# Rotating images by 90 degrees: loads of 16 rows to a partition, two images alternating on a quadrant's partitions, in slabs of 2 MB

## The chip, the cores and the metric

One core of a Trainium2 chip runs the kernel; the launch names no other. The metric is the device time of one execution in microseconds (us). Medians of several runs are given. "Span" is the length of the profiled execution, about 1.8 us less than the time of the same run.

## The reference

```python
x = np.random.randn(32, 3, 256, 256).astype(np.float32)      # 25.17 MB
out = np.rot90(x, k=-1, axes=(-2, -1))                       # out[.., i, j] = x[.., 255 - j, i]
```

Nothing is computed. Every byte is read once and written once, and each of the 96 images is transposed with one axis reversed.

## The kernel before

```python
R = 8; G = H // R                      # 8 rows of an image on a partition; 32 partitions = 1 image
n_slabs = B * C * G // P               # 24 slabs of 4 images, 1 MB
PARTS = 2; CP = R // PARTS
ld_v = x.rearrange("b c h w -> (b c h) w").rearrange("(n p r) w -> n p (r w)", p=P, r=R)
st_v = out.rearrange("b c h w -> (b c h) w").rearrange("(n p c) w -> n p (c w)", p=P, c=R)
in_pool = ...bufs=12
out_pool = ...bufs=12

for n in range(n_slabs):
    t_in = in_pool.tile([P, R * W], fp32, tag="t_in")
    nc.sync.dma_start(out=t_in, in_=ld_v[n])              # 128 partitions x 8 KB
    t_out = out_pool.tile([P, R * W], fp32, tag="t_out")
    src = t_in.rearrange("p (r g c) -> p c r g", r=R, c=R)
    dst = t_out.rearrange("p (c g r) -> p c r g", c=R, r=R)[:, :, ::-1, ::-1]
    for k in range(PARTS):
        cs = slice(k * CP, (k + 1) * CP)
        nc.vector.transpose(out=dst[:, cs], in_=src[:, cs])   # 32x32 blocks on VectorE
    nc.scalar.dma_start(out=st_v[n], in_=t_out)           # 128 partitions x 8 KB
# ... (cut: imports, launch)
```

As the kernels use it, a transpose on VectorE swaps 32 partitions (called a quadrant here) with 32 elements of a partition. Here the 32 partitions are the 32 groups of 8 rows of one image, and the 32 elements are one column out of each of 32 groups of 8 columns, 32 bytes apart. So an output partition receives 8 whole output rows, 8 KB in one piece. In the traces no load or store is issued before the last one on its completion semaphore has landed; from the second use of a semaphore on, a load's issue starts 16 to 81 ns after that landing. Loads and stores use four semaphores each once stores run, so at most four loads and four stores are in flight. (At the very start five loads were issued before one had landed.)

## Time and profile before

| | before |
|---|---|
| time, median of 3 runs | 124.81 us |
| span of the profile | 122.9 us |
| VectorE busy | 94.6 us |
| data packets | 3072 loads and 3072 stores of 8 KB, 309 ns nearly all |
| end of the last load packet | 110.6 us |
| first packet, end of the last packet | 1.80 us, 121.61 us |

The packet counts and times are from the trace's record of each DMA packet. Below are lines of the page of the kernel before. DVE is VectorE. The first three are the 40 slices of the span (busy tenths of VectorE, busy tenths of the DMA engines, GB/s); then the two queues (q1 loads, q10 stores: packets, MB, share of 16 engines' span); then the chain of waits by engine; then the group of the transposes (count, busy us, mean ns of one, idle before it and what ended it).

```profile
DVE  0199999999897697796977967979769779797500
...
DMA  2999999999999999999999999999999999999994
GB/s 93 427 427 403 339 424 427 427 429 427 427 432 427 427 427 427 432 429 427 427 427 427 429 427 427 427 427 429 427 427 427 427 429 427 427 429 427 427 424 171
...
q1 hardware_dynamic: 3456, 25.17, 49.2%
q10 hardware_dynamic: 3456, 25.17, 48.5%
...
DMA 89%; DVE 2%; DVEq 2%; SPq 1%; issue 0%
...
L51 DVE STREAM_TRANSPOSE t_out<-t_in 128x1024 f32<-128x1024 f32 x48 | 94.6, 2052 | 20.9 <-DMA t_in<-in_x_dram 15.4
```

What to see: the DMA engines are at 9 tenths in every slice but the first and the last, at 427 GB/s nearly everywhere, while VectorE has gaps. The two queues together take 97.7% of the span. The waits of VectorE say the same (columns: who waited for what, us in total, times, longest):

```profile
DVE t_out L51 <- DMA t_in<-in_x_dram: 15.4, 12, 5.7
```

The arithmetic is short: 6144 packets x 309 ns / 16 engines = 118.7 us out of a span of 122.9 us. Only what makes packets cheaper, or the unused ends shorter, can shorten this kernel.

### The profile page before, as it was taken

The page shows a single profiled execution, that of the slowest core. Times are in us where ns is not written, and L with a number is a line of the kernel's source. Part 1 is how long each engine was busy: PE and PEld are TensorE (multiplying, and loading weights), DVE is VectorE, ACT ScalarE, POOL GpSimd, SP SyncE. Part 2 cuts the span into 40 slices and gives each one's busy share as a digit, 9 for nine tenths or more (in the row PEclk, how much of TensorE's full clock was granted, in tenths as well). Part 3 has the DMA queues.
Part 4 walks back from the last instruction along what each step waited for, and adds up shares of the span by engine and source line. Part 5 has one row for each costly group of instructions (what it writes and reads, how often), then busy time and mean ns, then how long its engine had stood idle before and what let it go on. Part 6 is the DMA issues. An engine that isn't in the chain of part 4 may idle for free.

```text
span 122.9 us, 186 instructions
## 1 busy us (share of the span) xinstructions
DVE 94.6 (77%) x48; POOL 0.2 (0%) x4
## 2 busy tenths in 40 slices
DVE  0199999999897697796977967979769779797500
POOL 0000000000000000000000000000000000000000
DMA  2999999999999999999999999999999999999994
GB/s 93 427 427 403 339 424 427 427 429 427 427 432 427 427 427 427 432 429 427 427 427 427 429 427 427 427 427 429 427 427 427 427 429 427 427 429 427 427 424 171
DMA packets 6913, 50.34 MB, mean 410 GB/s; under 512 B 768, under 2 KB 768, under 8 KB 768
## 3 DMA queue, kind: packets, MB, share of 16 engines
q1 hardware_dynamic: 3456, 25.17, 49.2%
q10 hardware_dynamic: 3456, 25.17, 48.5%
q14 instruction: 1, 0.01, 0.0%
HBM read 25.17 MB, written 25.17 MB: 410 GB/s over the span
## 4 chain that ended last, share of the span: by engine, by line
DMA 89%; DVE 2%; DVEq 2%; SPq 1%; issue 0%
DMA t_in<-in_x_dram 89%; DVE t_out L51 2%; DVEq L79 2%; SPq L44 1%; DVEq L51 0%
## 5 line engine op out<-in xcount | busy, mean ns | idle before, releaser
L51 DVE STREAM_TRANSPOSE t_out<-t_in 128x1024 f32<-128x1024 f32 x48 | 94.6, 2052 | 20.9 <-DMA t_in<-in_x_dram 15.4
L68 POOL MEMSET const-uint8-127<- 128x1 uint8 x1 | 0.1, 102 | 0.0
L68 POOL MEMSET const-bfloat16-1.0<- 128x1 bf16 x1 | 0.1, 101 | 0.0
L68 POOL MEMSET const-float32-0.0<- 128x1 f32 x1 | 0.1, 98 | 0.2 <-issue 0.2
L68 POOL MEMSET const-float32-1.0<- 128x1 f32 x1 | 0.1, 98 | 0.0
## 6 DMA issues: line engine op xcount, KB each, us to landing
t_in<-in_x_dram SPq DMA_DIRECT2D x24, 1024.0 KB, 19.6
out_dram<-t_out ACTq DMA_DIRECT2D x24, 1024.0 KB, 16.5
```

What stands on the lines that cost most here:

```text
L44: nc.sync.dma_start(out=t_in, in_=ld_v[n])
L51: nc.vector.transpose(out=dst[:, cs], in_=src[:, cs])
L68: nc = _bacc.Bacc("TRN2", target_bir_lowering=False, num_devices=1)
L79: with _tile.TileContext(nc) as tc:
```

## The change

The intent is fewer and larger load packets. Sixteen rows of an image lie in one piece of 16 KB, so a partition is loaded by one packet of 16 KB. An image then takes only 16 partitions, and since a quadrant has 32, two images share it, on alternating partitions. Each load therefore writes every second partition, 64 in all. After the transpose, the two images' pixels alternate along the free axis, and the output access pattern sorts them into two halves of the output tile. Stores stay at 8 KB a partition.

```diff
-    R = 8
-    G = H // R
-    n_slabs = B * C * G // P
-    PARTS = 2
-    CP = R // PARTS
+    RI, RO = 16, 8
+    K, G = H // RI, H // RO
+    I = 2
+    Q = P // (K * I)
+    n_slabs = B * C // (Q * I)
...
+    ld_v = ...rearrange("(n i m r) w -> n i m (r w)", i=I, m=Q * K, r=RI)
+    st_v = ...rearrange("(n i p c) w -> n i p (c w)", i=I, p=P, c=RO)
-    in_pool = ...bufs=12        # the same for out_pool
+    in_pool = ...bufs=6
...
-        t_in = in_pool.tile([P, R * W], fp32, tag="t_in")
-        nc.sync.dma_start(out=t_in, in_=ld_v[n])
+        t_in = in_pool.tile([P, RI * W], fp32, tag="t_in")
+        for i in range(I):
+            nc.sync.dma_start(out=t_in[i::I], in_=ld_v[n, i])
...
+        t_out = out_pool.tile([P, I, RO * W], fp32, tag="t_out")
+        src = t_in.rearrange("p (r g c) -> p c r g", r=RI, c=RO)
+        dst = t_out.rearrange("p i (c k r) -> p c r k i", c=RO, r=RI)[:, :, ::-1, ::-1, :]
+        for c in range(RO):
+            nc.vector.transpose(out=dst[:, c], in_=src[:, c])
-        nc.scalar.dma_start(out=st_v[n], in_=t_out)
+        for i in range(I):
+            nc.scalar.dma_start(out=st_v[n, i], in_=t_out[:, i])
```

More of the change, by code (lines that the diff above doesn't have):

```diff
@@ L29 @@
     P = nc.NUM_PARTITIONS
-    R = 8
-    G = H // R
-    n_slabs = B * C * G // P
-    PARTS = 2
-    CP = R // PARTS
-    ld_v = x.rearrange("b c h w -> (b c h) w").rearrange("(n p r) w -> n p (r w)", p=P, r=R)
-    st_v = out.rearrange("b c h w -> (b c h) w").rearrange("(n p c) w -> n p (c w)", p=P, c=R)
-    in_pool = ctx.enter_context(tc.tile_pool(name="in_pool", bufs=12))
-    out_pool = ctx.enter_context(tc.tile_pool(name="out_pool", bufs=12))
-    for n in range(n_slabs):
-        t_in = in_pool.tile([P, R * W], fp32, tag="t_in")
-        nc.sync.dma_start(out=t_in, in_=ld_v[n])
-        t_out = out_pool.tile([P, R * W], fp32, tag="t_out")
-        src = t_in.rearrange("p (r g c) -> p c r g", r=R, c=R)
-        dst = t_out.rearrange("p (c g r) -> p c r g", c=R, r=R)[:, :, ::-1, ::-1]
-        for k in range(PARTS):
-            cs = slice(k * CP, (k + 1) * CP)
-            nc.vector.transpose(out=dst[:, cs], in_=src[:, cs])
-        nc.scalar.dma_start(out=st_v[n], in_=t_out)
+    RI, RO = 16, 8
[3 more added lines that the diff above has]
+    n_slabs = B * C // (Q * I)
+    ld_v = x.rearrange("b c h w -> (b c h) w").rearrange(
+        "(n i m r) w -> n i m (r w)", i=I, m=Q * K, r=RI)
+    st_v = out.rearrange("b c h w -> (b c h) w").rearrange(
+        "(n i p c) w -> n i p (c w)", i=I, p=P, c=RO)
+    in_pool = ctx.enter_context(tc.tile_pool(name="in_pool", bufs=6))
+    out_pool = ctx.enter_context(tc.tile_pool(name="out_pool", bufs=6))
+    for n in range(n_slabs):
+        t_in = in_pool.tile([P, RI * W], fp32, tag="t_in")
[8 more added lines that the diff above has]
+            nc.scalar.dma_start(out=st_v[n, i], in_=t_out[:, i])
 _INS = ['x']
```

## The prediction

> **What bounds it now.** The DMA engines. The page's 40 slices show DMA at 9 tenths from the second to the last but one, at 424 to 432 GB/s; the two queues took 49.2% and 48.5% of the 16 engines' span. Almost every 8 KB packet took 309 ns, so 6144 packets on 16 engines are 118.7 us; the rest is about 4 us of start, slow early packets and end, and 1.9 us by which the time exceeds the profile's span. The chain of waits agrees: 89% is load DMA. VectorE is busy 94.6 us (77%); its idle time (20.9 us) is mostly waiting for loads. Back to back, 128x1024 transposes start 1.907 us apart.
>
> In every 4 us window loads and stores move equally many packets (about 104)[...].
>
> **What changes.**
> 1. Bytes, DMA count (24 loads, 24 stores of 1 MB), pool bytes and DMAs in flight stay.
> 2. Load packets become 16 KB, half as many. 8 KB in 309 ns is 26.5 GB/s[...].
> 3. [...] Loads run ahead, stores lag; the total stays. The store backlog at the end (VectorE finishing near 105 us) hides the larger last slab (8 us of transposes, 4.9 us of stores). Worth about 0.
> 4. VectorE: 96 transposes of 512 elements per partition instead of 48 of 1024; [...]97 us in all, off the path. The first transpose waits for 2 MB: about 8 us instead of 5.7, off the path too.
> 5. The transposes' writes alternate between two halves 8 KB apart, then step 64 bytes, instead of stepping 32 bytes. If a write costs the same, nothing follows. There is little room: about 8 us per 2 MB slab now, and by my sum (8 + 12 slabs + 5 for the last stores + 3) VectorE binds above about 9 us.
> 6. Each load writes every second partition. [...]
>
> **Prediction.** 125.0 us, essentially unchanged; 123.4 to 142 should hold it 8 times in 10. Faster by over 2%: 0.06; within 2%: 0.56; slower by over 2%: 0.38. The long upper side is points 5 and 6.
>
> **What would show it.** Right: DMA at 9 tenths to the end; 16 KB load packets at about 610 ns, store packets at 309; loads done near 85 to 100 us, then stores alone at about 427 GB/s; transposes 0.95 to 1.05 us apart; the chain ending in store DMA. Wrong by 5: transposes over 1.13 us apart, VectorE busy nearly all of the span, DMA slices below 9, VectorE as the chain. Wrong by 6: load packets much above 618 ns while GB/s falls in the first slices, where loads run alone. Wrong by 3: a DMA gap before the last two stores. If packets of 16 KB are cut to 8 KB or less, points 2 and 3 vanish and the result stays near 125.
>
> **What would make it wrong.** A write-side penalty of the transposes with the 8 KB alternation (over 12%), [...]or loads stalling on buffers while too few stores are queued.

In point 2 is a saving of 0.8 us; with it the sum of the forecast came to 124.8 - 0.8 = 124.0 us, and the point of 125.0 leaned upward from there. The loads and stores are equal in packets on average only (0.998:1): from 20 to 104 us of the trace 96 to 114 load packets and 97 to 113 store packets end in each.

## The result, and the profile after

| | before | after |
|---|---|---|
| time, median of 6 runs | 124.83 us | 124.55 us |
| span of the profile | 122.9 us | 122.9 us |
| VectorE busy | 94.6 us | 96.3 us |
| load packets | 3072 of 8 KB, 309 ns | 1536 of 16 KB, 611 ns |
| busy per DMA engine (sum of packets / 16) | 119.98 us | 119.48 us |
| end of the last load packet | 110.6 us | 85.5 us |
| first packet, end of the last packet | 1.80, 121.61 us | 2.04, 121.73 us |

The ratio is 0.9979, with a 95% interval of 0.9966 to 0.9992. (A ratio here is the mean time of one kernel's fast runs over that of the other's of the same rounds, so it is not quite the ratio of the medians.) The time is the same within 2%; the small gain is clear of zero. The single profiled execution does not show it: its span equals that of before, and two profiles of the changed kernel, this one and a later one (122.6 us), differ by more than the gain. The outputs are right.

The same lines of the page, after:

```profile
DVE  0029999999999999999999999999999999000000
...
DMA  3999999999999999999999999999999999999993
GB/s 85 427 427 427 427 427 365 400 437 413 424 448 432 413 427 451 429 389 435 424 461 437 408 427 437 427 424 421 427 427 429 429 427 427 427 427 427 427 427 139
...
q1 hardware_dynamic: 1920, 25.17, 48.8%
q10 hardware_dynamic: 3456, 25.17, 48.5%
...
DMA 58%; DVE 23%; DVEq 1%; issue 1%; SPq 0%; ACTq 0%
...
L53 DVE STREAM_TRANSPOSE t_out<-t_in 128x512 f32<-128x512 f32 x96 | 96.3, 1092 | 8.4 <-DMA t_in<-in_x_dram 8.4
```

and the same view of VectorE's waits:

```profile
DVE t_out L53 <- DMA t_in<-in_x_dram: 8.4, 1, 8.4
```

What to see: the DMA line is the same as before, 9 tenths from end to end, and that is the result. What changed is the order. VectorE now runs without a gap from 8 us to 105 us (it waits once, for the first slab), then has nothing left to do, while the DMA engines are still at 427 GB/s with stores alone. The chain of waits now gives VectorE 23% instead of 2%; the experiments show below that this is not a bound.

### The profile page after: what moved, and what is told of

The parts are those of the page before. It is cut to its first block, busy times and chain, and to the rows that moved or that the text cites. A ratio compares the mean times of both kernels' runs of the same rounds, so it can differ in the third digit from the quotient of the medians.

```text
span 122.9 us, 225 instructions
## 1 busy us (share of the span) xinstructions
DVE 96.3 (78%) x96; POOL 0.2 (0%) x4
## 3 DMA queue, kind: packets, MB, share of 16 engines
q1 hardware_dynamic: 1920, 25.17, 48.8%
q10 hardware_dynamic: 3456, 25.17, 48.5%
HBM read 25.17 MB, written 25.17 MB: 410 GB/s over the span
## 4 chain that ended last, share of the span: by engine, by line
DMA 58%; DVE 23%; DVEq 1%; issue 1%; SPq 0%; ACTq 0%
DMA out_dram<-t_out 53%; DVE t_out L53 23%; DMA t_in<-in_x_dram 6%; DVEq L82 1%; SPq L47 0%; ACTq L56 0%; DVEq L53 0%
## 5 line engine op out<-in xcount | busy, mean ns | idle before, releaser
L53 DVE STREAM_TRANSPOSE t_out<-t_in 128x512 f32<-128x512 f32 x96 | 96.3, 1092 | 8.4 <-DMA t_in<-in_x_dram 8.4
```

The source lines that it names most:

```text
L53: nc.vector.transpose(out=dst[:, c], in_=src[:, c])
```

## The experiments

"Wrong on purpose" means that rows land in other places than the reference wants, while sizes, counts and instructions stay as told.

### 1. Only the transposes cut in two

```diff
 # kernel before
-    PARTS = 2
+    PARTS = 4
```

> The kernel before with only its transposes cut into 48x2 of 512 elements per partition (four per slab), writes still stepping 32 bytes. Theory: the fixed cost of an instruction alone explains the spacing after the change, so back-to-back starts are about 1.00 us apart (1001 ns after the change, 1907/2 = 954 plus 47). VectorE busy about 96 us, time 124.8 (124.6 to 125.0), since it is off the path. Rival: the 8 KB alternation of the writes costs something; then this kernel's spacing is clearly below 1001 ns, near 954 to 980.

Measured: 124.75 us, ratio to before 0.9993 (0.9978 to 1.0008). Back-to-back starts are 984 ns apart. The page's group line:

```profile
L51 DVE STREAM_TRANSPOSE t_out<-t_in 128x512 f32<-128x512 f32 x96 | 97.0, 1104 | 18.7 <-DMA t_in<-in_x_dram 13.1
```

That is between the theory (1001) and the rival (954 to 980): of the 47 ns, cutting costs 984 - 1907/2 = 30 ns an instruction, and the remaining 17 ns (1001 in the changed kernel) belong to the new shape. Whether its alternating writes cause them was not tested apart. In experiment 3 the writes alternate too, but the reads alternate between two images 16 KB apart and step 64 bytes instead of 32; there the starts are 920 ns apart (VectorE busy 89.4 us). So the pattern of the reads, or of both sides together, can matter more than these 17 ns. A VectorE busy time 2 us longer (97.0 against 94.6) moved nothing, as it should off the path. The prediction's cost of cutting was a guess, and too high; 30 ns is what was measured.

### 2. The change with load packets of 8 KB

```diff
 # changed kernel; wrong result on purpose
-        "(n i m r) w -> n i m (r w)", i=I, m=Q * K, r=RI)
+        "(n i b m r) w -> n i m b (r w)", i=I, m=Q * K, b=2, r=RI // 2)
...
-            nc.sync.dma_start(out=t_in[i::I], in_=ld_v[n, i])
+            nc.sync.dma_start(out=t_in[i::I].rearrange("p (b f) -> p b f", b=2), in_=ld_v[n, i])
```

> The changed kernel, with each load's 16 KB per partition read as two pieces of 8 KB from places far apart in the source (wrong result on purpose; everything else as changed). Theory (the packet size is what saves, and what moves the sharing): load packets of 8 KB at 309 ns, busy time per engine up by 0.67 us, loads and stores again equal in packets, loads end near 110 us instead of 85.5, VectorE starved again; time 125.2 (124.9 to 125.6), because at 1:1 the stores still lag by the 7.8 MB loaded before the first store, 18 us, enough to hide the last slab. Rival A (the saving comes from slab size or order, not packets): time stays at 124.55. Rival B (run-ahead[...] is needed to hide the larger last slab): a gap in DMA at the end and 126.5 us or more.

Measured: 125.24 us, ratio to before 1.0034 (1.0021 to 1.0048). Load packets are 8 KB at 309 ns; the engines' busy time is 120.35 us instead of 119.48; loads and stores are equal in bytes again (0.997 between 24 and 104 us and 0.998 before; the changed kernel has 1.79 between 24 and 84 us, while loads last); loads end at 104.7 us, not near 110 as expected. The slices and the waits:

```profile
DVE  0029999999999999999994994994995997798000
...
DMA  3999999999999999999999999999999999999993
```

```profile
DVE t_out L53 <- DMA t_in<-in_x_dram: 16.8, 6, 8.6
```

VectorE has gaps again, waiting for loads, while the DMA line stays full. So the packet size gives the saving and moves the sharing; with 8 KB packets the rest is a small loss (the first packet came at 2.19 us instead of 1.80 before; 0.15 us of that is this variant's own, since the changed kernel has 2.04). And the slab of 2 MB is hidden at its end even at 1:1: rival B falls.

### 3. 16 KB packets on both sides

Two more images share each input partition, so that a transposed block has two images on its output partitions too, with 16 output rows each.

```diff
 # changed kernel
-    RI, RO = 16, 8
+    RI, RO = 16, 16
-    I = 2
+    I, J = 2, 2
-    n_slabs = B * C // (Q * I)
+    n_slabs = B * C // (Q * I * J)
-        "(n i m r) w -> n i m (r w)", i=I, m=Q * K, r=RI)
+        "(n i j m r) w -> n i j m (r w)", i=I, j=J, m=Q * K, r=RI)
-        "(n i p c) w -> n i p (c w)", i=I, p=P, c=RO)
+        "(n i j m c) w -> n i j m (c w)", i=I, j=J, m=Q * G, c=RO)
     # both pools: bufs=3; t_in is [P, J, RI * W]
-            nc.sync.dma_start(out=t_in[i::I], in_=ld_v[n, i])
+            for j in range(J):
+                nc.sync.dma_start(out=t_in[i::I, j], in_=ld_v[n, i, j])
-        src = t_in.rearrange("p (r g c) -> p c r g", r=RI, c=RO)
+        src = t_in.rearrange("p j (r g c) -> p c r g j", r=RI, c=RO)
-            nc.scalar.dma_start(out=st_v[n, i], in_=t_out[:, i])
+            for j in range(J):
+                nc.scalar.dma_start(out=st_v[n, i, j], in_=t_out[j::J, i])
```

> Loads and stores both of 16 KB a partition: two images alternate on the input partitions and two more share each partition, so that output partitions hold 16 rows too; slabs of 4 MB, 3 + 3 buffers. Theory: packets of 611 ns on both queues, another 0.67 us less engine time, sharing 1:1; loads end later than 85.5; time 123.9 (123.6 to 124.2). Rival (the larger slab exposes its start or its end[...]): no gain or worse, 124.6 to 128, with a gap in DMA or store packets clearly over 618 ns.

Measured: correct, 124.26 us, ratio to before 0.9964 (0.9946 to 0.9981). Both kinds of packet take 611 ns, and the busy time per engine is 118.86 us: 0.62 us less than the change, as expected. The time gained only about half of that (0.29 us by the medians), just outside the range. To settle it, the two ran again on one chip, five rounds each:

> The changed kernel again, as the partner of the next run on the same chip: 0.2 to 0.4 us under the kernel before.

> 16 KB on both sides again, on the same chip as the changed kernel. Theory (0.6 us less engine time, of which 0.49 us was seen at the last packet): 0.3 to 0.6 us under the changed kernel, 0.6 to 0.9 us under the kernel before. Rival: no difference from the changed kernel beyond 0.1 us.

Measured in these rounds: before 124.70 us, changed kernel 124.52 us (ratio 0.9985, 0.9971 to 0.9999), 16 KB on both sides 124.24 us (ratio 0.9961, 0.9946 to 0.9976). It beats the changed kernel by 0.28 us and the kernel before by 0.46 us, both less than I expected (0.3 to 0.6 and 0.6 to 0.9). One reason is that the sum of the packets' times overstates the saving. Sixteen engines that each took 309 ns for one 8 KB packet after another would move 424.2 GB/s. With each packet's bytes spread over its own time, the records of the kernel before give 427.5 GB/s between 40 and 80 us. So records of successive packets overlap by about 0.8% (the DMA share reads 1.01 in that window), and the rate is the better measure. With 16 KB on both sides it is 430.6 GB/s (90 to 118 us, in both profiles). At these rates 25.17 MB of loads, or of stores, take 0.43 us less with 16 KB packets, not 0.67; this is an estimate. What became of the rest (0.43 against 0.28 us) was not settled.

### 4. Load packets of 32 KB, and the same cut to 8 KB

```diff
 # changed kernel
-    RI, RO = 16, 8
+    RI, RO = 32, 8
-    I = 2
+    I = 4
     # slabs of 4 MB, so both pools: bufs=3
```

> Loads of 32 KB a partition (four images alternating, four loads of 32 partitions a slab), stores still 8 KB; slabs of 4 MB, 3 + 3 buffers. Theory: load packets of 32 KB at about 1213 ns, 0.35 us less engine time than the change[...]; time 124.2 (123.9 to 124.6). Rivals: packets are capped at 16 KB or less (time 124.5); or loads run into their three buffers and DMA falls idle before stores exist (time over 125).

Measured: correct, 128.53 us, ratio 1.0286 (1.0261 to 1.0312). The packets are not capped: 32 KB take 1213 ns. But the time is 4 us worse. The slices and the waits:

```profile
DVE  0000899999999999998079999169999999991000
...
DMA  4799898999899999989999999999999999916995
GB/s 165 331 496 444 382 496 351 475 496 331 351 418 426 416 426 418 475 380 426 393 431 426 442 442 403 421 423 439 424 421 434 423 421 436 423 41 248 413 421 240
```

```profile
DVE t_out L53 <- DMA t_in<-in_x_dram: 13.3, 1, 13.3
DVE t_out L53 <- issue: 8.3, 2, 4.4
```

The second rival (an idle DMA) has the right sign, but names the wrong place and cause. The DMA hole is near the end, at 111 to 114 us (41 GB/s in that slice). VectorE stood still twice, 8.3 us in all. The waits view calls that "issue", which names no releaser. The chain of waits in order of time (start, length, what) and the timeline from 60 us on (start, length, what, idle before) tell more:

```profile
30.37 33.65 DMA out_dram<-t_out
...
64.04 19.43 DMA out_dram<-t_out
```

```profile
64.20 15.59 DVE L53 STREAM_TRANSPOSE t_out<-t_in 128x1024 f32<-128x1024 f32 x8 [4.42 <-issue]
83.65 31.04 DVE L53 STREAM_TRANSPOSE t_out<-t_in 128x1024 f32<-128x1024 f32 x16 [3.87 <-issue]
```

Store DMAs end at 64.02 and 83.47 us, and transposes start 0.2 us after each; at the second of these the last load had landed 6 us before. So VectorE waited for output buffers that slow stores held. By 76 us only 6.0 MB had been stored. To see whether the packets or the 4 MB slabs did that, the same kernel ran with each load cut into 8 KB pieces:

```diff
 # the 32 KB kernel; wrong result on purpose
-        "(n i m r) w -> n i m (r w)", i=I, m=Q * K, r=RI)
+        "(n i b m r) w -> n i m b (r w)", i=I, m=Q * K, b=4, r=RI // 4)
     # and the load's destination viewed as "p (b f) -> p b f", b=4
```

> The kernel with 32 KB loads and 4 MB slabs, each load now read as four pieces of 8 KB from places far apart in the source (wrong result on purpose). Theory (in the 32 KB kernel [...]VectorE stood still for output buffers, 8.3 us, and the stores ran dry at the end): with packets 1:1 VectorE no longer waits for output buffers, no DMA gap near 110 us, engine time as in the 8 KB variant of the change; time 125.3 (124.9 to 125.9) instead of 128.5. Rival (the 4 MB slabs with three buffers cause the stall): about 128.5 again.

That the stores lagged is shown by the 6.0 MB above.

Measured: 124.88 us, ratio to before 1.0007 (0.999 to 1.0023).

```profile
DVE  0000699999999999999999999999945999940000
...
DMA  2999999999999999999999999999999999999993
```

```profile
DVE t_out L53 <- DMA t_in<-in_x_dram: 13.4, 1, 13.4
DVE t_out L53 <- issue: 3.1, 1, 3.1
```

By 76 us, 9.2 MB had been stored, the hole is gone, and VectorE ended at 109.5 us instead of 114.7. So it was the packets. The theory was not exact: a wait of 3.1 us for output buffers stays, but it comes early enough to cost nothing, and the time fell slightly below my range.

### 5. Loads on 64 neighbouring partitions

```diff
 # changed kernel; wrong result on purpose
-            nc.sync.dma_start(out=t_in[i::I], in_=ld_v[n, i])
+            nc.sync.dma_start(out=t_in[i * (P // I):(i + 1) * (P // I)], in_=ld_v[n, i])
```

> The changed kernel with each load on 64 neighbouring partitions (0 to 63, then 64 to 127) instead of every second one; wrong result on purpose, same bytes and packets. [...]load packets while loads run alone take about 1200 ns instead of 611 and the DMA moves about 214 GB/s there; time well above the change, 140 us or more. Rival[...]: packets stay at 611 ns and the time at 124.5.

The theory's figures stand for half the rate of the changed kernel's loads, and the half was the author's estimate.

Measured: 165.81 us, ratio 1.3302 (1.3228 to 1.3376). Where loads run alone, the rate is half. The windows of 4 to 16 us (from:to, length, VectorE, POOL, clock, DMA share, GB/s), first of the changed kernel, then of this one:

```profile
4.00:16.00 12.00, 7.64 (x8) 0.00 (x0) 1.00 1.01 429
```

```profile
4.00:16.00 12.00, 2.79 (x3) 0.00 (x0) 1.00 1.05 218
```

218 GB/s is half (51%) of the changed kernel's 429. The load packets between 8 and 16 us take 1258 ns on average instead of 611. Note that the DMA share reads full in both (1.01 and 1.05), so a packet's time in the trace grows as the rate falls, and a full DMA line does not prove a full rate. With stores beside them the rate is still only 303 GB/s (40 to 80 us). So the alternation is what keeps the change from being a large loss. Why neighbouring partitions halve the rate was not shown.

### 6. More VectorE work on purpose

```diff
 # changed kernel; the result stays right
-        for c in range(RO):
+        for c in list(range(RO)) + [0] * 1:      # then * 2
```

> The changed kernel with one transpose of each slab done twice: 9 instead of 8 per slab, so about 9.0 us a slab. Theory (VectorE is off the path with 8, and binds just about 9): VectorE ends at 8.4 + 12 x 9.0 = 116.5 us of the span, then 2 MB of stores: time 126 (124.5 to 127). Rival (VectorE is already on the path, as the 23% in the chain of waits may suggest): plus 12 us, 136.5.

> The same with two transposes of each slab done twice: 10.0 us a slab. Theory: VectorE binds; it ends at 8.4 + 12 x 10.0 = 128.5 us, then 4.9 us of stores and about 3 us of issue and completion, plus 1.7: time 138 (136.5 to 139.5); DMA slices fall below 9 in the second half. Rival (VectorE on the path from the start): 148.5, plus 24.

Measured: with 9 transposes a slab 125.88 us, ratio 1.0093 (1.0078 to 1.0108); with 10, 139.90 us, ratio 1.1214 (1.1198 to 1.1231). The slices of the first, then of the second:

```profile
DVE  0039999999999999999999999999999999999600
...
DMA  3999999999999999999999999999999999999495
GB/s 85 423 423 423 433 433 370 412 439 402 433 444 433 418 420 447 425 415 433 444 415 423 441 436 420 423 449 404 423 428 431 425 428 431 425 428 428 188 415 222
```

```profile
DVE  0059999999999999999999999999999999999900
...
DMA  3999999999999999999999999999997076086086
GB/s 119 423 442 418 433 414 354 437 418 437 425 418 440 428 425 430 433 433 418 421 440 435 416 442 416 423 425 435 425 425 330 0 321 288 0 342 266 0 359 250
```

Twelve more transposes are about 12 us of VectorE work and cost 1.3 us; the next twelve cost 14 us. That is a bound that takes over. In the first run VectorE ends at 116.8 us and the last store packet at 122.85 us, 6.06 us later; in the second it is 130.67 and 136.7 us, 6.04 us later (and 1.2 us more to the end of the span in each). The DMA-bound end is 121.7 us, so by estimate (121.7 less these 6.0) VectorE may end up to 115.7 us of the span before it costs anything; in the changed kernel it ends at 104.7 us. Over 12 slabs that is a margin of 0.9 us on 8.0. The second run fell 0.4 us outside my range, because a slab took 10.2 us instead of the 10.0 I had reckoned with. And the 23% of the chain of waits did not mean that VectorE was on the path: with it, the first run would have taken 12 us more.

### 7. Fewer input buffers

```diff
 # changed kernel
-    in_pool = ...bufs=6
+    in_pool = ...bufs=2        # then 3
```

> The changed kernel with 2 input buffers of 2 MB instead of 6. Theory: the two buffers are full at 11.9 us, and no load can start until the first slab's transposes end at 16.4 us, and no store until then either: a DMA gap of about 4.5 to 5.5 us near the start, which is never made up; afterwards DMA is busy and the time is 129.5 (128.5 to 131). It shows that a larger slab is harmless only while loads can fill the DMA during the first slab. Rival: the gap is made up later and the time stays within 1 us of 124.5, which would mean that DMA work is not the bound.

Measured: 139.09 us, ratio 1.1131 (1.1057 to 1.1205). The expected gap is there, but the expected size is far off.

```profile
DVE  0059999159999059999129999408999808999900
...
DMA  4995099999999999998999999899989999999486
GB/s 105 429 448 238 0 305 329 462 396 453 405 408 343 441 450 396 422 322 334 410 441 422 422 343 379 362 429 427 400 343 334 346 398 439 450 405 419 181 360 250
```

```profile
DVE t_out L53 <- DMA t_in<-in_x_dram: 21.9, 4, 8.3
DVE t_out L53 <- DMA out_dram<-t_out: 11.4, 2, 5.8
```

My theory had one gap and then a full DMA line. In fact DMA stalls recur: over the run the engines are idle for at least 8.3 us between packets (the time from first to last packet less the sum of their times), and their packets take 6.6 us more in sum per engine than in the changed kernel (load packets 661 ns on average, store packets 324). VectorE waits for loads (21.9 us) and for output buffers (11.4 us).

> The changed kernel with 3 input buffers instead of 6 (2 gave 139). Theory: three buffers are filled just when the first slab's transposes end, 16.4 us, so no first gap; and a slab's load then has two slabs of transposes, 16 us, to land, so VectorE never waits for it: time 124.6 (124.3 to 125.2). Rival (any loss of run-ahead costs): between 126 and 135.

Measured: 125.79 us, ratio to before 1.0091 (1.0074 to 1.0108), against 124.52 us for six buffers on the same chip. That lies between the theory's range and the rival's. The slices:

```profile
DMA  2999999999999999999999999999999999999993
GB/s 79 429 423 429 429 357 333 392 373 437 423 437 423 442 431 434 423 423 410 437 423 429 439 450 402 445 418 445 410 431 423 426 423 429 431 426 423 426 434 161
```

VectorE waits once, for the first slab, exactly as with six, and the DMA line has no gap, but the rate dips (333 GB/s in one slice). Still it is 1.27 us slower. Of that, 0.87 us per engine are longer packets (120.26 us busy against 119.39): between 16 and 24 us, when loads resume and stores begin together, load packets average 717 ns and store packets 381 ns. Why packets stretch when traffic of both kinds begins at once was not settled. Both kernels pay some of it (the load packets' excess over their usual time sums to 0.86 us per engine before, and to 1.06 and 0.97 us in the two profiles after).

## Why the prediction was right

The time, 124.55 us, lies in the range, in the class predicted ("within 2%"), 0.45 us below the point. Point by point:

1. **Bytes, DMA count, DMAs in flight unchanged.** Right, apart from six loads instead of five at the very start, and up to six stores instead of four at the end.
2. **Larger packets save 0.8 us.** The direction is right (experiment 2: 125.24 us with 8 KB load packets against 124.55). The size, an estimate, was about twice too large. The packets' own times fall by 192 x 309 ns - 96 x 611 ns = 0.67 us per engine, but these records overlap; by the rates of experiment 3 the estimate is 0.43 us. The prediction also missed the start: the first load's issue takes 521 ns instead of 372, and the first packet moves from 1.80 to 2.04 us. In sum: -0.43 + 0.24 gives about -0.2 us; the medians say -0.28, and in the rounds of experiment 3 -0.18. The prediction's point of 125.0 was above the sum of its own terms (124.8 - 0.8 = 124.0); it leaned upward for the risks of points 5 and 6, which did not come. So that the point came within 0.45 us is partly luck: the measured time lies between the sum and the point, about as far from each.
3. **Loads run ahead, stores lag; worth 0.** Right. Loads were ahead by 1.79:1 in bytes (24 to 84 us) and ended at 85.5 us; the stores alone ran at 427 GB/s to the end; the last slab is hidden, as it is at 1:1 (experiment 2). What the traces show is 0.998:1 in bytes in the kernel before and 0.997:1 in the 8 KB variant, with equal packets, and 1.79:1 with 16 KB against 8 KB, which is 0.9 load packets to one store packet; why it is 1.79 is open. What I did not foresee is that more of the same can be bad: with 32 KB the stores lag so far that VectorE blocks on output buffers and a hole follows (experiment 4).
4. **VectorE 97 us, first transpose at about 8 us, end near 105 us.** Right: 96.3, 8.36 and 104.7 us. Cutting cost 30 ns an instruction, less than guessed; the new shape added 17 ns, so the sum (47 ns) nearly hit by chance.
5. **VectorE binds above about 9 us a slab; the 8 KB alternation might cost.** The threshold is right (about 8.9 us by experiment 6). The new shape, alternation included, costs 17 ns on 984, under 2%; the alternation was not timed by itself.
6. **Writing every second partition might stretch the load packets.** It did not: 611 ns, and 429 GB/s between 4 and 16 us. Writing 64 neighbouring ones did: 1258 ns and 218 GB/s (experiment 5).

## What to carry to other kernels

The DMA line here was full from end to end, before and after at 427 GB/s between 40 and 80 us, and only time per byte and the two ends counted: a change of order that ended VectorE's gaps was worth nothing, and a larger packet was worth a few ns each (an estimate: at 427.5 and 430.6 GB/s, 16 KB on one of 16 engines take 613.2 and 608.8 ns, 4 to 5 ns less as one packet than as two). Packet size also moved how the two busy queues shared the engines (0.998:1 in bytes with 8 KB on both, 1.79:1 with 16 KB loads), and with 32 KB loads, 6.0 MB stored by 76 us against 9.2 with the same loads cut to 8 KB, a change to loads alone starved the stores; keep an eye on the buffers behind them. Before blaming an engine that has grown in the chain of waits, add work to it: here 12 us more on it cost 1.3 us.

## What else the traces show of the hardware

- Loads of 64 partitions ran at full rate where they took every second one: 429 GB/s against 218 GB/s for 64 neighbours.
- Packets of 8, 16 and 32 KB took 309, 611 and 1213 ns: 602 ns for the 16 KB between the last two, so by estimate (309 x 2 - 611, 611 x 2 - 1213) 7 to 9 ns a packet beyond the bytes. By the rates (427.5 and 430.6 GB/s) it is 4 to 5 ns, since packet records overlap.
- The issue time of a DMA by shape: the first load of 128 x 8 KB took 372 ns on the queue, of 64 x 16 KB 521 ns, of 64 x 2 x 8 KB 677 ns (the usual load later on: 328, 472 and 602 ns), and the first packet moved with it (1.80, 2.04, 2.19 us).
- VectorE's time for 32-bit transposes with strides: 1907 ns from start to start for 1024 elements a partition with both sides stepping 32 bytes, and 30 ns for cutting one in two.
- Packets stretched when loads resumed and stores began together (717 and 381 ns on average with three input buffers, 16 to 24 us); the cause is open.
